# Spacing numbers, two buffer counts and one bank string changed in the hybrid layer of a three-layer kernel

## Chip, core and metric

The kernel runs on one core of one Trainium2 chip. The metric is the device time of one execution in microseconds (us), from the first instruction to the last. The engines are PE (TensorE, matrix products), DVE (VectorE), ACT (ScalarE), POOL (GpSimd) and SP (SyncE, which here only issues DMA transfers).

## What is computed

Three transformer layers run over 256 tokens of width 1024: a layer with sliding-window attention and a dense feed-forward, a layer with forgetting attention and eight experts, and a "hybrid" layer with 32 small experts. Only the hybrid mixer is touched:

```python
def hybrid_mixer(x, ...):
    proj = x @ w_in                                   # 1024 -> 6912 columns
    y_a = rwkv7_mixer(proj[..., :OFF_MOBA], ...)      # recurrence over the tokens, 8 heads of 64
    y_b = moba_attention(q, k, v)                     # attention, 8 heads of 64
    y_c = s5_mixer(proj[..., OFF_SSM:OFF_GATE], ...)  # state space model, 32 groups of 16 channels
    gates = sigmoid(proj[..., OFF_GATE:] + gate_b)    # three gates of 1024 columns
    merged = gates[0] * (y_a @ w_up_rwkv) + gates[1] * (y_b @ w_up_moba) + gates[2] * (y_c @ w_up_ssm)
    return merged @ w_out
```

The recurrence of `rwkv7_mixer` is S <- S*w + (S a) b' + v k', y = S r for each head and token. The kernel does it in chunks of 64 tokens: two blocks of 128 tokens (`tb` 0 and 1), each with two chunks.

## The kernel before

The weights of the whole program stream through SBUF in parts of 128 x 1024 numbers, in the order of a plan that is made ahead. A part is loaded into a raw buffer (tile `wr`), and where it is wanted in two halves, `_split` writes them into a split buffer (tile `ws`): ACT copies the high half (L123), DVE subtracts it and leaves the low half (L124). Four raw and three split buffers are there all the time; `k.room(nraw, nsplit, k.part_b)` adds some for the parts that lie in the plan ahead of `part_b`. A load or a split is issued as soon as a buffer of its kind has been released by the order of the program, so the number of buffers sets how early a split stands in the queues of ACT and DVE. Every engine takes its own queue strictly in order.

A projection (`gemm`) of 512 columns takes 12 PE instructions of 128x512 for each part, 6 for each half of the tokens; below, "dense" rows are those, on `bank_g`. The eight PSUM banks are shared out by letter: in part A `bank_g` (three), `bank_a` (two) and `bank_t` (three), in part B g=4, t=2, y=2.

The hybrid layer has two parts. In each, `weave(main, *sides, lat)` writes one order for all engines from a main generator of dense work and side generators of small dependent steps. A side that says `yield t` is resumed once the program's own count of PE time (`k.pe.us`, a sum by operand shapes, made while the program is built) has grown by `lat * t`. When the main generator is used up, what is left of the sides is written behind it, with nothing between its steps.

- Part A: `weave(dense(), att, states(), lat=1.0)`. Main is the attention's projections (`mb`), the S5 input `u2` (`inputs()`) and the recurrence's inputs (`z2`); the sides are the attention and the S5 scan (L1780 to L1809).
- Part B: `weave(dense2(), r.steps, r.ahead, lat=0.7)`. Main is the gates, the S5 output (`glu`) and two of the three up projections. The sides are the recurrence: `early(tb)` (decays; exponentials L1993 to L1995, a product with `rind`, normalised keys), `late(tb)` (products `rkt` L2042 and `rbt` L2043, then four turns by PE, called T(rt), T(at), T(rkt), T(rbt) here), `recur(tb)` (products rarT x rbT and rarT x rkT, a matrix inverse by levels with L2137 ahead of the first, then for each chunk W, copy L2170, U, copy L2178, state H and output y) and `finish(tb)` (group norm of y, L2216 to L2234, then the turn T(ry)). `r.ahead` is `early(1)`; `r.steps` is all the rest, `finish(0)` being resumed inside `recur(1)`.

Behind part B the up projection of the recurrence's output (`up0`, on tiles `hyr` that T(ry) and two copies fill) and the output projection `o2` follow, and then the 32 experts, whose weights (`wx`) fill large buffers; more of these open once the buffers of `o2` are closed.

Of the kernel before, what the change touches and what calls it, by code (L numbers as in the profile page):

```python
# [385 lines left out]
def through(gen):  # L386
    for _ in gen:
        pass
# [30 lines left out]
def until(ready, *what):  # L419

    n = 0
    while not all(w in ready for w in what):
        n += 1
        assert n < 10000, what
        yield 0.5
# [179 lines left out]
class Attention:  # L605
# [73 lines left out]
    def steps(self, units):  # L679

        def start(u):
            if "prep" in u:
                yield from u["prep"]
            self.scores(u)

        yield from start(units[0])
        self.soft(units[0])
        yield 5.0
        for n, u in enumerate(units):
            more = n + 1 < len(units)  # L690
            if more:
                yield from start(units[n + 1])
            yield 2.0
            self.turn(u)
            if more:
                self.soft(units[n + 1])
            yield 2.0
            self.values(u)
            if "after" in u:
                u["after"]()  # L700
            yield 2.5
# [900 lines left out]
class Ssm:  # L1602
# [47 lines left out]
    def tile(self, shape, name, bufs=1, dt=F32):  # L1650
        return self.pool.tile(shape, dt, name=name, tag=name, bufs=bufs)
# [206 lines left out]
class Rwkv:  # L1858
# [97 lines left out]
    def early(self, tb, tile):  # L1956

        k, nc, row = self.k, self.k.nc, self.row
        z = self.z[:, tb]
        hd = lambda v: v.rearrange("p (h d) -> p h d", h=8)  # L1960
        wide = lambda v: v.rearrange("p (h o) -> p h o", o=1).to_broadcast([128, 8, 64])
        v = self.of[tb] = {}
        g = v["g"] = self.tile([128, 512], "rg", 2)
        PC = v["PC"] = self.tile([128, 4, 2], "rPC", 2)
        nc.scalar.activation(z[:, 1536:1600], z[:, 1536:1600], AF.Tanh)
        nc.scalar.activation(z[:, 1664:1792], z[:, 1664:1792], AF.Sigmoid)
        lt = self.tile([128, 2, 128], "rlt2")
        yield 1.5
        p = k.t()
        for i in range(2):  # L1970
            k.pe.transpose(p[:, i * 128:i * 128 + 128], z[:, 1536 + i * 128:1664 + i * 128], k.ident)
        k.copy(lt, p[:, :256].rearrange("p (i t) -> p i t", i=2))
        yield 1.5
        sw, a, kk = (tile(i) for i in (6, 7, 3))
        p, p2 = k.t(), k.t()
        k.pe.matmul(p, lt[0:64, 0], self.wa[0:64], start=True, stop=True)
        k.pe.matmul(p2, lt[64:128, 0], self.wa[64:128], start=True, stop=True)
        nc.vector.tensor_add(sw, p, row["w0"])
        nc.vector.tensor_add(a, p2, row["a0"])
        nc.scalar.activation(sw, sw, AF.Sigmoid)  # L1980
        nc.scalar.activation(a, a, AF.Sigmoid)
        kv, r = z[:, 512:1024], z[:, 0:512]
        nc.vector.tensor_mul(kk, kv, row["k_k"])
        yield 2.0
        p = k.t()
        k.pe.matmul(p, lt[:, 1], self.g2, start=True, stop=True)
        nc.scalar.copy(g, p)
        yield 2.0
        E = [tile(i) for i in range(3)]
        p, p2 = k.t(), k.t()  # L1990
        k.pe.matmul(p, self.upto, sw, start=True, stop=True)
        k.pe.matmul(p2, self.before, sw, start=True, stop=True)
        nc.scalar.activation(E[0], p, AF.Exp, scale=-KAPPA)  # L1993
        nc.scalar.activation(E[1], p, AF.Exp, scale=KAPPA)
        nc.scalar.activation(E[2], p2, AF.Exp, scale=-KAPPA)  # L1995
        yield 1.5
        p = k.t()
        for j in range(4):
            k.pe.matmul(p[:, 2 * j:2 * j + 2], sw[:, j * 128:j * 128 + 128], self.ind, start=True, stop=True)
        nc.scalar.activation(PC, p[:, :8].rearrange("p (j c) -> p j c", c=2), AF.Exp, scale=-KAPPA)  # L2000

        sq = sw
        nc.gpsimd.tensor_mul(sq, kk, kk)
        yield 1.5
        s8 = self.tile([128, 3, 8], "rs8", 2)
        nc.vector.tensor_reduce(out=s8[:, 0], in_=hd(sq), op=OP.add, axis=AX.X)
        nc.gpsimd.tensor_scalar(s8[:, 0], s8[:, 0], 1e-24, None, op0=OP.max)
        nc.gpsimd.tensor_tensor(s8[:, 1], s8[:, 0], k.neghalf.to_broadcast([128, 8]), op=OP.pow)
        rt, at = E[0], E[2]
        nc.vector.tensor_mul(rt, r, rt)  # L2010

        kn = kv
        nc.vector.scalar_tensor_tensor(sq, a, -1.0, row["k_a"], op0=OP.add, op1=OP.mult)
        nc.vector.scalar_tensor_tensor(kn, sq, 1.0, kv, op0=OP.add, op1=OP.mult)
        yield 3.0
        nc.vector.tensor_mul(hd(kk), hd(kk), wide(s8[:, 1]))
        nc.vector.scalar_tensor_tensor(at, kk, -1.0, at, op0=OP.mult, op1=OP.mult)
        nc.gpsimd.tensor_mul(a, kk, a)
        v.update(rt=rt, at=at, a=a, E=E[1], kn=kn)
        yield 2.0  # L2020
        self.ready.add(tb)

    def late(self, tb):

        k, nc, row = self.k, self.k.nc, self.row
        hd = lambda v: v.rearrange("p (h d) -> p h d", h=8)
        v = self.of[tb]
        self.bt = self.tile([128, 512], "rbt")
        self.kt = self.tile([128, 512], "rkt")
        self.arT = self.tile([128, 4, 2, 128], "rarT")  # L2030
        self.bT = self.tile([128, 4, 128], "rbT")
        self.kT = self.tile([128, 4, 128], "rkT")
        bonus = v["bonus"] = self.tile([128, 8], "rbonus", 2)
        self.PC = v["PC"]

        def turned(src, dst):
            p = k.t()
            for j in range(4):
                k.pe.transpose(p[:, j * 128:j * 128 + 128], src[:, j * 128:j * 128 + 128], k.ident)
            k.copy(dst, p.rearrange("p (j t) -> p j t", j=4))  # L2040

        nc.vector.tensor_mul(self.kt, v["kn"], v["E"])  # L2042
        nc.gpsimd.tensor_mul(self.bt, v["a"], v["E"])  # L2043
        turned(v["rt"], self.arT[:, :, 1])
        yield 1.0
        turned(v["at"], self.arT[:, :, 0])
        yield 1.5
        turned(self.kt, self.kT)
        yield 1.5
        turned(self.bt, self.bT)  # L2050
        kn = v["kn"]
        nc.gpsimd.tensor_mul(kn, kn, row["r_k"])
        nc.gpsimd.tensor_mul(kn, kn, self.z[:, tb, 0:512])
        yield 2.0
        nc.vector.tensor_reduce(out=bonus, in_=hd(kn), op=OP.add, axis=AX.X)

    def steps(self, yh, yl):
        yield from self.early(0, lambda i: self.tile([128, 512], f"ru{i}"))
        yield from self.late(0)
        yield from self.recur(0)  # L2060
        end = self.finish(0, yh, yl)
        next(end)
        yield from until(self.ready, 1)
        yield from self.late(1)
        for i, t in enumerate(self.recur(1)):
            if i in (1, 4):
                next(end, None)
            yield t
        yield from self.finish(1, yh, yl)
# [24 lines left out]
    def recur(self, tb):  # L2094
        k, nc = self.k, self.k.nc
# [30 lines left out]
        def level(l):  # L2126
            t = tl([128, 2, 4, 64], "ru5" if l % 2 else "ru8")
            nc.gpsimd.tensor_mul(f(t), f(NT), lv(self.level[:, l]))
            return t
# [6 lines left out]
        products(MN, lambda u, hs: self.eye[hs], p)  # L2136
        nc.vector.tensor_add(f(X), pv(p), lv(self.eye))  # L2137
        MN = level(1)
        yield 2.0
        for l in range(1, 6):  # L2140
            p = k.t()
            products(MN, lambda u, hs: f(X)[hs, u], p)
# [102 lines left out]
ALPHA2 = 2.0 ** 0.25  # L2245
NIN = 6912
MOBA_BUFS = 1
MORE_A = (2, 0)
LAT_A, LAT_B = 1.0, 0.7
ZCHUNKS = ((1536, 256), (512, 512), (0, 512), (1024, 512))  # L2250

# [101 lines left out]
def hybrid(k, A, x, before, scratch, spare, extra):  # L2353
    nc, tc = k.nc, k.tc
    with ExitStack() as hy:
# [18 lines left out]
        with ExitStack() as pa:  # L2374
# [17 lines left out]
            ep = es.enter_context(k.pool(name="rws", side="right"))  # L2392
            close = k.room(*MORE_A, k.part_b)
            through(islice(g, 2))
# [7 lines left out]
            r.constants()  # L2402

            def inputs():
                ps = [k.bank(b) for b in "gggt"]
                yield from turned_gemm(k, "u2", xh, xl, 512, ps)
                us = ep.tile([128, 4, 4, 64], F32, name="hus")
                for b in range(4):
                    k.copy(us[:, b], ps[b][:, :256].rearrange("p (n t) -> p t n", t=4))
                for h, e in enumerate((nc.vector, nc.gpsimd)):  # L2410
                    for t in range(4):
                        for c in range(4):
                            e.tensor_copy(uT[h][32 * t:32 * t + 32].rearrange("p (b c) n -> p b c n", c=4)[:, :, c],
                                          us[32 * c:32 * c + 32, 2 * h:2 * h + 2, t])
                ready.add("u")
# [507 lines left out]
```

## Time before, and its profile

| | |
|---|---|
| median of 3 runs | 1864.01 us (1863.45 to 1866.99) |
| profiled execution | 1866.05 us, span 1864.3 us |
| mean granted PE clock | 0.971 of full speed |
| PE busy over the span | 1730.8 us, 93% |
| DVE, ACT, POOL busy | 718.0, 455.7, 363.9 us (39%, 24%, 20%) |
| part A (1244 to 1384 us) | 140 us, PE busy 128.64 |
| part B (1384 to 1577 us) | 193 us, PE busy 175.64 |

PE is the busiest engine in every stage shown. Its idle time within a stage is what other engines or transfers make it wait for, and the profile names the instruction that released it.

### The profile page before, as it was taken

The page shows a single profiled execution, that of the slowest core. Times are in us where ns is not written, and L with a number is a line of the kernel's source. Part 1 is how long each engine was busy: PE and PEld are TensorE (multiplying, and loading weights), DVE is VectorE, ACT ScalarE, POOL GpSimd, SP SyncE. Part 2 cuts the span into 40 slices and gives each one's busy share as a digit, 9 for nine tenths or more (in the row PEclk, how much of TensorE's full clock was granted, in tenths as well). Part 3 has the DMA queues.
Part 4 walks back from the last instruction along what each step waited for, and adds up shares of the span by engine and source line. Part 5 has one row for each costly group of instructions (what it writes and reads, how often), then busy time and mean ns, then how long its engine had stood idle before and what let it go on. Part 6 is the DMA issues. An engine that isn't in the chain of part 4 may idle for free. (4 is left out here: it accounts for less than half of the span.)

```text
span 1864.3 us, 41874 instructions
## 1 busy us (share of the span) xinstructions
PE 1730.8 (93%) x18607; PEld 1197.5 (64%) x18607; DVE 718.0 (39%) x1147; ACT 455.7 (24%) x791; POOL 363.9 (20%) x622
## 2 busy tenths in 40 slices
PE   8989999899899999999999999989889989889776
PEld 7867888788645464646464656578767767665343
DVE  5558655654501020202112020247677565621102
ACT  5534444355210000000000000024344333311001
POOL 4410989400100000000000000036234142000000
PEclk9999999999999999999999999989999999989889
DMA  7515676544579999999999999855564235989996
GB/s 226 154 57 186 199 231 207 172 115 165 221 300 381 409 379 405 383 405 384 406 383 394 393 383 405 324 195 162 169 185 130 81 87 168 363 353 419 419 418 233
DMA packets 126483, 514.97 MB, mean 276 GB/s; under 512 B 21148, under 2 KB 50250, under 8 KB 88916
## 3 DMA queue, kind: packets, MB, share of 16 engines
q1 hardware_dynamic: 123012, 496.35, 70.7%
q0 software_dynamic: 3280, 15.83, 2.6%
q8 instruction: 150, 2.46, 0.5%
q14 instruction: 41, 0.34, 0.1%
HBM read 502.44 MB, written 7.87 MB: 274 GB/s over the span
## 5 line engine op out<-in xcount | busy, mean ns | idle before, releaser
L232 PE MATMUL bank_r<-wl,gx 128*32 128x352 f32 x6144 | 459.4, 460 | 2.5 <-ACTq L1357 2.5
L232 PE MATMUL bank_g<-ws,xh 128*128 128x256 f32 (+2 forms) x1440 | 389.4, 351 | 14.5 <-DVE ws L124 5.2
L232 PEld LDWEIGHTS bank_r<-wl,gx 128*32 128x32 f32 x6144 | 217.9, 110 | 237.3 <-issue 140.0
L124 DVE TENSOR_TENSOR ws<-wr,ws 128x1024 fp32r<-128x1024 f32 (+1 forms) x200 | 256.9, 1294 | 156.9 <-ACT ws L123 156.5
L232 PEld LDWEIGHTS bank_g<-ws,xh 128*128 128x128 f32 x1440 | 257.3, 196 | 54.6 <-DVE ws L124 7.9
L123 ACT ACTIVATE ws<-wr 128x1024 fp32r<-128x1024 f32 (+1 forms) x200 | 209.6, 1058 | 205.0 <-PE bank_g L232 113.9
L232 PE MATMUL bank_g<-ws,xl 128*128 128x256 f32 (+2 forms) x720 | 236.2, 344 | 3.3 <-DVE xl L363 3.1
L232 PE MATMUL bank_r<-wl,ehT 128*32 128x256 f32 x4224 | 231.4, 379 | 4.2 <-DVE ehT L1445 4.0
L232 PEld LDWEIGHTS bank_r<-wl,ehT 128*32 128x32 f32 x4224 | 161.2, 110 | 72.2 <-issue 8.9
L1444 DVE TENSOR_TENSOR eh<-eh,bank_r 128x352 f32<-128x352 f32 x48 | 22.9, 504 | 428.7 <-PE bank_r L232 428.1
L566 POOL TENSOR_TENSOR lnmv<-lnmv,neghalf 128x1 f32<-128x1 f32 x10 | 10.0, 1000 | 822.1 <-DVE lnmv L565 822.1
L232 PEld LDWEIGHTS bank_g<-ws,xl 128*128 128x128 f32 x720 | 141.1, 196 | 17.5 <-DVE xl L363 4.1
L1467 ACT CAST ey<-bank_r 128x256 fp32r<-128x256 f32 x24 | 8.9, 373 | 415.5 <-PE bank_r L232 414.6
L232 PE MATMUL bank_g<-wx,x 128*32 128x256 f32 x784 | 71.2, 433 | 15.6 <-DMA wx<-in_expert_w_gate_dram 14.4
L1468 DVE TENSOR_TENSOR ey<-bank_r,ey 128x256 fp32r<-128x256 f32 x24 | 10.1, 424 | 165.0 <-ACT ey L1467 164.9
L1438 ACT ACTIVATE eh<-bank_r 128x352 f32<-128x352 f32 x48 | 22.3, 465 | 206.7 <-PE bank_r L232 201.6
L232 PEld LDWEIGHTS bank_g<-wx,x 128*32 128x32 f32 x784 | 32.7, 123 | 45.6 <-DMA wx<-in_expert_w_gate_dram 19.1
L650 POOL TENSOR_TENSOR aP<-aP,ast 128x512 f32<-128x512 f32 (+1 forms) x20 | 24.4, 1219 | 175.6 <-DVE ast L648 133.9
L232 PE MATMUL bank_g<-ws,hh 128*128 128x512 f32 x176 | 57.5, 399 | 0.0
L232 PE MATMUL bank_g<-ws,oh 128*128 128x512 f32 x128 | 44.4, 409 | 0.0
L1445 DVE STREAM_TRANSPOSE ehT<-eh 128x704 f32<-128x704 f32 x24 | 43.0, 1792 | 0.8
L583 POOL TENSOR_TENSOR lnmv<-lnmv,neghalf 128x1 f32<-128x1 f32 x2 | 1.1, 558 | 205.4 <-DVE lnmv L582 205.4
(715 smaller groups left out, 2202.8 us busy)
## 6 DMA issues: line engine op xcount, KB each, us to landing
wl<-in_w_exp_in_dram SPq DMA_DIRECT2D x128, 1408.0 KB, 8.8
wl<-in_w_exp_out_dram SPq DMA_DIRECT2D x64, 1408.0 KB, 8.4
wr<-in_w_in_dram SPq DMA_DIRECT2D x54, 512.0 KB, 3.8
wx<-in_expert_w_up_dram SPq DMA_DIRECT2D x25, 1024.0 KB, 19.9
wx<-in_expert_w_gate_dram SPq DMA_DIRECT2D x24, 1024.0 KB, 19.9
wx<-in_expert_w_down_dram SPq DMA_DIRECT2D x23, 1024.0 KB, 19.9
wr<-in_w_ffn_in_dram SPq DMA_DIRECT2D x44, 512.0 KB, 4.1
wr<-in_w_out_dram SPq DMA_DIRECT2D x24, 512.0 KB, 4.3
```

The costliest lines, as they stand in the source:

```text
L123: nc.scalar.activation(hv, v, AF.Copy)
L124: nc.vector.tensor_sub(lv, v, hv.bitcast(F32))
L232: self.nc.tensor.matmul(out, lhsT, rhs, start=start, stop=stop)
L566: nc.gpsimd.tensor_tensor(mv[:, 3:4], mv[:, 2:3], self.k.neghalf, op=OP.pow)
L583: nc.gpsimd.tensor_tensor(mv[:, 3:4], mv[:, 2:3], self.k.neghalf, op=OP.pow)
L650: e.tensor_mul(P[:, hs, :nk], P[:, hs, :nk], st[:, 3, hs].rearrange("p (h o) -> p h o", o=1).to_broadcast([128, 2, nk]))
L1438: nc.scalar.activation(h[:, g, s * H2:s * H2 + H2], pa[g][s], AF.Silu)
L1444: nc.vector.tensor_mul(v, v, pb[g][s])
L1445: nc.vector.transpose(hT[:, g], h[:, g].rearrange("p (r j) -> p j r", j=KF))
L1467: nc.scalar.copy(y[:, 0, g], ps[g])
L1468: nc.vector.tensor_sub(y[:, 1, g], ps[g], y[:, 0, g].bitcast(F32))
```

## The change

```diff
--- before.py
+++ after.py
@@ -1993,7 +1993,7 @@
         nc.scalar.activation(E[0], p, AF.Exp, scale=-KAPPA)
         nc.scalar.activation(E[1], p, AF.Exp, scale=KAPPA)
         nc.scalar.activation(E[2], p2, AF.Exp, scale=-KAPPA)
-        yield 1.5
+        yield 8.0
         p = k.t()
         for j in range(4):
             k.pe.matmul(p[:, 2 * j:2 * j + 2], sw[:, j * 128:j * 128 + 128], self.ind, start=True, stop=True)
@@ -2044,9 +2044,9 @@
         turned(v["rt"], self.arT[:, :, 1])
         yield 1.0
         turned(v["at"], self.arT[:, :, 0])
-        yield 1.5
+        yield 4.0
         turned(self.kt, self.kT)
-        yield 1.5
+        yield 4.0
         turned(self.bt, self.bT)
         kn = v["kn"]
         nc.gpsimd.tensor_mul(kn, kn, row["r_k"])
@@ -2063,7 +2063,7 @@
         yield from until(self.ready, 1)
         yield from self.late(1)
         for i, t in enumerate(self.recur(1)):
-            if i in (1, 4):
+            if i in (4, 7):
                 next(end, None)
             yield t
         yield from self.finish(1, yh, yl)
@@ -2136,7 +2136,7 @@
         products(MN, lambda u, hs: self.eye[hs], p)
         nc.vector.tensor_add(f(X), pv(p), lv(self.eye))
         MN = level(1)
-        yield 2.0
+        yield 4.0
         for l in range(1, 6):
             p = k.t()
             products(MN, lambda u, hs: f(X)[hs, u], p)
@@ -2245,7 +2245,7 @@
 ALPHA2 = 2.0 ** 0.25
 NIN = 6912
 MOBA_BUFS = 1
-MORE_A = (2, 0)
+MORE_A = (0, 1)
 LAT_A, LAT_B = 1.0, 0.7
 ZCHUNKS = ((1536, 256), (512, 512), (0, 512), (1024, 512))
 
@@ -2402,7 +2402,7 @@
             r.constants()
 
             def inputs():
-                ps = [k.bank(b) for b in "gggt"]
+                ps = [k.bank(b) for b in "ggtt"]
                 yield from turned_gemm(k, "u2", xh, xl, 512, ps)
                 us = ep.tile([128, 4, 4, 64], F32, name="hus")
                 for b in range(4):
```

Four spacing numbers, a pair of step numbers, a pair of buffer counts and one string change. `yield` values grow in `early` (behind the exponentials), `late` (ahead of T(rkt) and T(rbt)) and `recur` (ahead of the first level's products), and `finish(0)` is resumed at the steps 4 and 7 of `recur(1)` instead of 1 and 4. `MORE_A` gives part A one more split buffer in place of two more raw ones: 4 raw and 4 split instead of 6 and 3. The `u2` projection puts its third block of 128 columns on a `bank_t` instead of a `bank_g`. No instruction is added or removed by it; the order of every engine's queue changes.

The first place is DVE's queue at the start of part A, where the splits begin (`L334` is a copy of attention values; the numbers behind `ws_` and `wr_` only tell tiles apart).

```order
 L363 TENSOR_TENSOR xl<-bank_t,xh 128x4x128 x2
-L124 TENSOR_TENSOR ws_12575<-wr_12041,ws_12575 128x1024
-L124 TENSOR_TENSOR ws_12580<-wr_12565,ws_12580 128x1024
-L124 TENSOR_TENSOR ws_12617<-wr_12567,ws_12617 128x1024
+L124 TENSOR_TENSOR ws_12571<-wr_12041,ws_12571 128x1024
+L124 TENSOR_TENSOR ws_12576<-wr_12565,ws_12576 128x1024
+L124 TENSOR_TENSOR ws_12581<-wr_12567,ws_12581 128x1024
+L124 TENSOR_TENSOR ws_12618<-wr_12569,ws_12618 128x1024
 L334 COPY hmb_12366<-bank_g 128x256
```

Four splits stand ahead of the first copy instead of three, and so on through part A: each split stands one part earlier, until the last one.

The second place is PE's queue at the start of part B, from the two products with `sw` (`rupto`, `rbefore`) on. Before:

```order
L232 MATMUL bank_t<-ru_13808,rupto 128x512
L232 MATMUL bank_t<-ru_13808,rbefore 128x512
L232 MATMUL bank_g<-ws_13797,xh 128x512
L232 MATMUL bank_g<-ws_13797,xl 128x512
L232 MATMUL bank_g<-ws_13797,xh 128x512
L232 MATMUL bank_g<-ws_13797,xl 128x512
L232 MATMUL bank_g<-ws_13797,xh 128x512 x2
L232 MATMUL bank_t<-rind,ru_13808 128x2 x4
```

With the change:

```order
L232 MATMUL bank_t<-ru_13808,rupto 128x512
L232 MATMUL bank_t<-ru_13808,rbefore 128x512
L232 MATMUL bank_g<-ws_13797,xh 128x512
L232 MATMUL bank_g<-ws_13797,xl 128x512
L232 MATMUL bank_g<-ws_13797,xh 128x512
L232 MATMUL bank_g<-ws_13797,xl 128x512
L232 MATMUL bank_g<-ws_13797,xh 128x512 x2
L232 MATMUL bank_g<-ws_13826,xh 128x512
```

The product with `rind`, 6 dense instructions behind `rbefore` in the one, comes 24 dense instructions later in the other. In the same way T(rkt) and T(rbt) have 18 dense instructions ahead of them instead of 6 in both blocks, and the first level's products in the second block 18 in place of 12.

The third place is PE's queue at the end of part B. Before, these rows stand ahead of the last T(ry), and 34 dense instructions more ahead of them, back to the last product of `recur(1)` on `bank_y`:

```order
L232 MATMUL bank_g<-ws_15566,xh 128x512 x2
L232 MATMUL bank_g<-ws_15598,xh 128x512
L232 MATMUL bank_g<-ws_15598,xl 128x512
L232 MATMUL bank_g<-ws_15598,xh 128x512
L232 MATMUL bank_g<-ws_15598,xl 128x512
L232 MATMUL bank_g<-ws_15598,xh 128x512 x2
L236 MATMUL bank_t<-ident,ry 128x128 x4
```

With the change:

```order
L232 MATMUL bank_y<-rUc,ru_15023 64x64
L232 MATMUL bank_y<-rHc,rarT 64x64
L232 MATMUL bank_y<-rz,ru_15025 64x64
L232 MATMUL bank_y<-rUc,ru_15023 64x64
L236 MATMUL bank_t<-ident,ry 128x128 x4
L232 MATMUL bank_g<-ws_15380,hyr_13750 128x512
L232 MATMUL bank_g<-ws_15380,hyr_13751 128x512
```

All dense rows of part B now stand ahead of the last 16 products on `bank_y` of the level steps; from there to T(ry) the recurrence's steps follow each other (W, U, H and y of chunk 0, then W, U and y of chunk 1), and behind T(ry) come `up0`'s rows with `hyr`.

## Rows read from the trace of the kernel before

**Rows 1.** Windows A, B: us; PE, PEld, DVE, ACT, POOL busy us; PE clock, DMA share, GB/s.
```profile
1244.00:1384.00 140.00, 128.64 (x895) 112.66 (x894) 95.69 (x128) 57.42 (x103) 66.02 (x109) 0.98 0.56 179
1384.00:1577.00 193.00, 175.64 (x2026) 136.29 (x2026) 121.70 (x161) 71.40 (x96) 65.87 (x51) 0.98 0.41 126
```

**Rows 2.** Waits of PE from 1270 to 1660: us in all, times, longest us.
```profile
PE bank_g L232 <- DVE ws L124: 5.2, 4, 4.1
PE bank_t L232 <- ACT ru L1994: 4.2, 1, 4.2
PE bank_t L236 <- DVE ry L2234: 3.5, 1, 3.5
PE bank_t L236 <- DVE rkt L2042: 3.1, 2, 1.8
PE bank_g L232 <- ACT hus L332: 2.8, 1, 2.8
PE bank_t L232 <- DVE ru L2137: 2.5, 1, 2.5
PE bank_t L236 <- POOL rbt L2043: 2.3, 1, 2.3
```

**Rows 3.** Timeline of DVE, then PE, around 1340: start, us, engine, line, tile.
```profile
1331.42 1.23 DVE L124 TENSOR_TENSOR ws<-wr,ws 128x1024 fp32r<-128x1024 f32 x1
1337.03 1.52 DVE L1806 TENSOR_TENSOR st<-sq,srot 128x504 f32<-128x504 f32 x1
...
1342.94 1.74 DVE L124 TENSOR_TENSOR ws<-wr,ws 128x1024 fp32r<-128x1024 f32 x1
...
1344.73 0.73 PE L232 MATMUL bank_g<-ws,xh 128*128 128x512 f32 x2 [4.06 <-DVE ws L124]
```

**Rows 4.** Windows of 4 us behind four gaps; columns as in rows 1.
```profile
1344.00:1348.00 4.00, 3.27 (x15) 2.81 (x16) 3.96 (x7) 1.17 (x2) 1.27 (x1) 0.67 0.43 131
...
1496.00:1500.00 4.00, 2.75 (x14) 2.38 (x15) 0.48 (x1) 2.04 (x4) 3.90 (x4) 1.00 0.65 189
1516.00:1520.00 4.00, 4.00 (x37) 3.41 (x33) 2.00 (x3) 2.64 (x4) 0.00 (x0) 0.57 0.35 122
1576.00:1580.00 4.00, 2.94 (x10) 2.49 (x11) 3.76 (x5) 0.17 (x1) 0.00 (x0) 0.69 0.22 53
```

**Rows 5.** Timeline of DVE and PE behind the u2 projection.
```profile
1281.01 5.19 DVE L2413 COPY huT<-hus 32x128 f32<-32x128 f32 x16
...
1287.82 2.34 PE L232 MATMUL bank_t<-huT,sBT 128*128 128x64 f32 x20
```

**Rows 6.** Timeline of PE and DVE at the start of part B.
```profile
1416.22 3.02 PE L232 MATMUL bank_g<-ws,hy 128*128 128x512 f32 x12
...
1417.43 0.68 DVE L334 COPY rbT<-bank_t 128x512 f32<-128x512 f32 x1
```

**Rows 7.** Timeline of PE, ACT, DVE and POOL at the end of part B.
```profile
1563.55 0.28 PE L232 MATMUL bank_y<-rUc,ru 64*64 64x64 f32 x2
...
1564.43 0.63 ACT L2216 COPY ry<-bank_y 128x256 f32<-128x256 f32 x2
...
1565.70 0.68 DVE L2221 TENSOR_REDUCE rgn<-ry 128x8 f32<-128x512 f32 x1
...
1570.49 1.67 POOL L2227 TENSOR_TENSOR rgn<-rgn,neghalf 128x8 f32<-128x8 f32 x1
...
1572.19 1.53 DVE L2231 TENSOR_TENSOR ry<-ry,rgn 128x512 f32<-128x512 f32 x1 [1.84 <-POOL rgn L2227]
...
1577.06 0.69 PE L236 MATMUL bank_t<-ident,ry 128*128 128x128 f32 x4 [3.50 <-DVE ry L2234]
```

**Rows 8.** Window of H and y of chunk 0, second block; columns as in rows 1.
```profile
1552.89:1555.53 2.64, 2.64 (x81) 2.57 (x81) 1.07 (x3) 0.00 (x0) 0.00 (x0) 1.00 1.01 425
```

**Rows 9.** All instructions of line L2170 in part B: duration min/median/max in ns.
```profile
L2170 DVE COPY rWc<-bank_t x4: 417/421/425, 1469.2 to 1558.4; 128x256 f32<-128x256 f32 x4
```

**Rows 10.** The chain that ended last, near its end: start, us, what.
```profile
1842.36 7.08 DMA wx<-in_expert_w_down_dram
```

## The prediction

> **What bounds the kernel now.** I read the stages first. In part A PE is busy for 128.64 of 140 us, in part B for 175.64 of 193 us, and no other engine comes near that [rows 1]. So a stage gets shorter only where PE waits, and 11.4 and 17.4 us are all there is to win. The table of PE's waits then says for what: seven causes hold most of it, each once or a few times [rows 2]. The reader should see that none of them is a transfer; all are results of DVE, ACT or POOL that come late for one row of PE's queue. Last I looked at where the hybrid layer's end goes. The chain of waits ends with a load of expert weights of 7.08 us [rows 10], and those loads are released by PE as it finishes with the buffers; so I let a shift of part B's end pass one to one to the end of the program.
>
> A second cost hangs on the waits. Behind the gap of 2.50 us the granted clock is 0.57 over the next 4 us, behind the one of 4.06 us 0.67, behind the one of 3.50 us 0.69, and behind the one of 2.35 us it is 1.00 [rows 2 to 4]. A window at 0.57 has lost 4 x 0.43 = 1.7 us of full-speed work, one at 0.67 1.3 us. So I count a gap of 2.5 us or more as its length and 1.3 to 1.7 us on top, and a shorter one as its length alone.
>
> **The change part by part.** No instruction is added, so the sum is made of waits that go, waits that come and the clock behind both.
>
> *The split buffer.* The longest split wait of part A is at 1344.73: PE has waited 4.06 us for a low half (L124) that starts at 1342.94, because on DVE it stands behind four operations of the S5 scan that began at 1337.03; the split before it ran at 1331.42 [rows 3]. With each split one part earlier, the half that PE wants at 1340.7 stands in the place of the one at 1331.42. The next half, which runs at 1342.94, is wanted only after the rest of that part and the S5 and attention products that PE's order has there, which need the scan's end themselves; I leave 0.3 us for that. Gain 3.8 us, and 1.3 us of clock: -5.1. Bounds: nothing (another split waits in its place, see below) and -5.8 (with the 1.7 us of clock). The two raw buffers that go cost nothing: a raw part is split as soon as it is there, the wait table names no load of `wr`, and DMA is busy at 0.56 [rows 1]; should that cover fail, one exposed split load would cost no more than the wait just removed.
>
> *The shared banks.* PE waits 2.8 us for ACT to copy a `bank_g` of `u2` [rows 2]. With a `bank_g` more at hand the next projection starts at once. But the S5 products that follow need `huT`, whose 16 copies on DVE run from 1281.01 for 5.19 us to 1286.2, and PE reached them at 1287.82 [rows 5]. PE can't pass 1286.4, so the gain is at most 1.4 us; the rest of the wait only moves there. I take -1.4; the lower bound is 0. The two parts of part A: -6.5.
>
> *Start of part B.* PE waits 4.2 us for the exponentials (L1994) and 1.8 us for `rkt` [rows 2], 6.0 in all, with a low clock behind the first. The change puts 24 dense instructions ahead of the `rind` product and 12 each ahead of T(rkt) and T(rbt). Twelve take 3.02 us [rows 6], so this is 6.0 + 3.0 + 3.0 us of cover, more than the waits are long. Against it: the dense rows that move bring their own splits with them, each 1.2 us of DVE [rows 3], ahead of the very operations the recurrence waits for. Three low halves instead of one stand ahead of the normalisation of the keys, and gate and S5 output sums (0.7 us each) come in ahead of L2017 and of the copy of `rbT` (L334, 0.68 us [rows 6]), for which the first product rarT x rbT waits. Walking DVE's and ACT's queues with the durations of the profile I find new waits of 1.4 us (a split behind the exponentials), 1.3 us at T(at), 1 us at T(rkt), 0.6 us in small pieces and 3.2 us ahead of rarT x rbT: 7.5 us against 6.0 + 1.7. I take 0. Bounds: -7.7 (every wait hidden) and +3.5 (the 3.2 us is a gap that brings the low clock and the rest grows by 2).
>
> *Second block.* Here `rkt` costs 1.23 us (3.1 less 1.85), `rbt` 2.3 and the first level (L2137) 2.5 with 1.7 of clock [rows 2, 4]. The dense rows put ahead are 3.0 us for each of the first two and 1.5 us for the third, whose own wait also starts from an emptier DVE queue. I take -3.1 for the two and -3.9 for the third, leaving 0.8 us of small waits: -7.0. Bounds -7.8 and -3.5 (cover of 1.5 us only for the third, the clock still falling behind the first two).
>
> *The end of part B.* The rows put ahead were taken from somewhere: the order has no dense row left between the last level step and T(ry). Two things are then bare. First the finish chain: from the last product of y, which ends at 1563.83, to T(ry) at 1577.06 it took 13.2 us [rows 7]: two copies on ACT, seven operations on DVE, three on POOL, one behind the other. It was covered by 42 dense rows, which is why PE waited only 3.50 us. With no split in DVE's and ACT's queues the copies start some 0.5 us sooner and L2221 follows them 0.4 us sooner: 12.3 us. Second, four copies between the last products, 0.42 us each [rows 9] and about 0.2 us to pass on the result and back, which dense rows covered: 2.5 us. Together 14.8 us bare for 3.5 before: +11.3; the low clock behind T(ry) is the same as now (0.69, [rows 4]). Bounds: +8 (the chain is a quarter shorter when nothing runs beside it: L2231 took 1.53 us where L2221, which reads as many numbers, took 0.68 [rows 7]) and +17 (below).
>
> *Sum:* -6.5 + 0 - 7.0 + 11.3 = -2.2 us. The profiled execution took 1866.05 us (its span of 1864.3 and 1.75 around it), so it would take 1863.85. It was 2.04 above the median of 1864.01; against the median I forecast 1861.8 us.
>
> **The rivals.** *The waits at the start of part B go too.* For it speaks that 12 us of cover stand against 6.0 us of waits and DVE is busy for only 121.70 of 193 us [rows 1]; against it, the order of DVE's queue, which puts splits and gate sums ahead of the wanted results. Then 6 of the 7.7 us are saved as well: 1855.8 us.
>
> *Slower: the bare end runs at the low clock.* From the last level step on PE has short products with gaps between them, which the trace nowhere shows for so long. H and y of the first chunk hold PE for 2.64 us [rows 8]; W and U of both chunks, y of the second and the last level step are about twice that again, so some 8 us at full clock (an estimate). If most of that runs at half speed it costs 6 us more, and with the 3.2 us gap at the start of part B followed by a low clock, 1.7: -2.2 + 7.7 = +5.5, 1869.5 us. It decides once more than about half of those products run slow. The page "TensorE: Matmul & The Clock Gate" of the Trainium skill, section "Loop structure matters more than you think", warns of just such a loop: it has the array go cold in a long wait between bursts and the next products run at the lower of the two clocks. By that rule alone the small products between short copies would stay fast and only the rows behind the 12 us gap be slow, as they are now; the trace agrees as far as it goes, with 0.69 behind 3.50 us and 1.00 behind 2.35 us.
>
> *Part A's stall only moves.* If the split at 1342.94 is still the one PE needs next, because the S5 products come later than I read, PE waits there instead: -5.1 becomes -1, and the sum +1.9: 1865.9 us.
>
> **How the numbers follow.** Forecast 0.45 (own range 1858.5 to 1865), first rival 0.2, second 0.2, third 0.15. A measurement of this kernel can tell about 0.2%, 3.7 us, from no change. Faster than 1860.3: the first rival and 0.35 of the forecast, 0.36. Slower than 1867.7: most of the second, a fifth of the third and a little of the forecast, 0.25. The rest, 0.39, is within 0.2%. The range leaves out one in ten on each side: 1854.5 to 1870.
>
> **What would show it.** In the profile after: no wait of 4 us for L124 in part A, and no window at 0.67 behind it; `huT` products reached some 1.4 us sooner, counted from `u2`; no wait for L1994, but new ones for L334 `rbT` in part B's first 45 us; no wait for `rbt` and at most 0.5 us for L2137; and one wait of 11 to 13 us for `ry` L2234 ahead of the last T(ry), with short ones for L2170 and L2178 ahead of it. I am wrong if that last wait is under 8 us, if the clock falls before it, or if the end of part B moves and the end of the program doesn't, because loads of expert weights set it by themselves.

## The result and the profile after

The changed kernel takes 1871.22 us in the median of 20 runs (1866.15 to 1881.61), the kernel before 1861.02 us in 20 runs on the same chips. The ratio is 1.0059, with a 95% interval of 1.0049 to 1.0070: slower, by some 11 us, where I had forecast 2.2 us less and a range that ended at 1870. The profiled execution has a span of 1873.0 us. The ratios and mean clocks below leave out two runs far off the rest (2467.70 us of a control, 5947.83 us of the kernel before).

The table of PE's waits from 1240 to 1660 us (in all, times, longest), to be laid beside [rows 2]:

```profile
PE bank_t L236 <- DVE ry L2234: 11.0, 1, 11.0
PE bank_g L232 <- ACT xxT L374: 6.5, 1, 6.5
PE bank_t L232 <- DVE ru L2113: 5.1, 1, 5.1
PE bank_g L232 <- DVE hmb L334: 4.2, 2, 2.3
PE bank_t L232 <- DVE hy L677: 3.9, 1, 3.9
...
PE bank_t L232 <- DVE rbT L334: 2.7, 1, 2.7
```

Every wait of [rows 2] that the change was aimed at is gone or smaller, and new ones stand in their places. The second row is the largest of those that no part of the prediction has. It lies behind part B, in the router of the experts (lines L2599 to L2623), which the diff does not touch. Timelines of ACT, SP and PE there in the changed kernel:

```profile
1635.65 2.02 ACT L2613 COPY xp<-x 128x1024 f32<-128x1024 f32 x1 [16.34 <-DVE x L571]
1637.58 1.06 ACT L374 COPY xxT<-bank_t 128x512 f32<-128x512 f32 x2
...
1628.54 0.58 SPq L2599 DMA_DIRECT2D xwr<-in_router_expert_w_dram  x1
1634.74 0.34 SPq L2602 DMA_DIRECT2D xrows<-in_ln_w_dram  x1
...
1635.79 1.28 SPq L192 DMA_DIRECT2D wx<-in_expert_w_gate_dram  x3
...
1638.21 2.13 PE L232 MATMUL bank_g<-xxT,xwr 128*36 128x128 f32 x9 [6.47 <-ACT xxT L374]
```

and in the kernel before:

```profile
1622.92 2.06 ACT L2613 COPY xp<-x 128x1024 f32<-128x1024 f32 x1 [9.89 <-DVE x L571]
...
1621.52 0.58 SPq L2599 DMA_DIRECT2D xwr<-in_router_expert_w_dram  x1
1622.20 0.62 SPq L2602 DMA_DIRECT2D xrows<-in_ln_w_dram  x1
...
1625.52 1.94 PE L232 MATMUL bank_g<-xxT,xwr 128*36 128x128 f32 x16
```

Before, the load of `xrows` follows that of `xwr` at once, and the copy follows the norm of the first 128 tokens. In the changed kernel ACT's copy of x into `xp` and SP's load of `xrows` both stand still until 1635, when DVE has finished the norm of the second 128 tokens. Behind ACT's copy queue the copies to `xxT` that PE wants, behind SP's load all further loads of expert weights.

To see where time goes I cut each trace at five places: the last copy L362 (part A begins), the first turn of `rz` by PE (part B's recurrence begins), the last T(ry), the load of `xrows`, and `xM` (the routing is known); a stage ends where the instruction named starts. The kernel before is a mean of three traces, one shown ahead and two controls:

| stage, us | before (3) | changed | overlap alone (2) | spacing alone (2) | all, one raw more |
|---|---|---|---|---|---|
| up to part A | 1245.9 | 1248.7 | 1245.3 | 1242.0 | 1243.8 |
| part A | 137.3 | 141.5 | 137.4 | 137.4 | 141.4 |
| part B to T(ry) | 196.3 | 199.9 | 195.8 | 200.8 | 200.1 |
| up0 and o2 to the xrows load | 44.0 | 44.7 | 49.7 | 38.3 | 38.8 |
| router to xM | 14.3 | 16.0 | 15.8 | 14.3 | 13.6 |
| experts | 225.0 | 222.3 | 224.1 | 225.9 | 225.5 |

The program ahead of part A and the experts vary by 3 and 5 us from run to run in the same kernel (1244.2 to 1247.3 and 222.9 to 227.8 in the three of before; ahead of part A, which the change does not touch, 1238.8 to 1248.7 over all fourteen traces), each of the four stages between by less than 1.5. Over these four the changed kernel takes 402.1 us for 391.9, 10.1 us more, about what the times say.

### The profile page after: what moved, and what is told of

It reads as the page before. It is cut to its first block, busy times and chain, and to the rows that moved or that the text cites. A ratio compares the mean times of both kernels' runs of the same rounds, so it can differ in the third digit from the quotient of the medians.

```text
span 1873.0 us, 41874 instructions
## 1 busy us (share of the span) xinstructions
PE 1728.0 (92%) x18607; PEld 1200.9 (64%) x18607; DVE 719.8 (38%) x1147; ACT 453.7 (24%) x791; POOL 365.3 (20%) x622
## 5 line engine op out<-in xcount | busy, mean ns | idle before, releaser
L124 DVE TENSOR_TENSOR ws<-wr,ws 128x1024 fp32r<-128x1024 f32 (+1 forms) x200 | 260.2, 1312 | 161.6 <-ACT ws L123 161.0
L1468 DVE TENSOR_TENSOR ey<-bank_r,ey 128x256 fp32r<-128x256 f32 x24 | 10.1, 424 | 164.8 <-ACT ey L1467 164.7
```

What stands on the lines that cost most here:

```text
L124: nc.vector.tensor_sub(lv, v, hv.bitcast(F32))
L1468: nc.vector.tensor_sub(y[:, 1, g], ps[g], y[:, 0, g].bitcast(F32))
```

## The experiments

The theory, formed on the two traces: the buffer counts lose the time, and they do it behind part B. The four raw buffers of the stream take turns. Two extra ones in part A or none leave the turn at another place when part A ends, and with it every later part lies in another buffer, up to the norm's weight and bias (L570 and L571 read them). Where the tiles lie in SBUF, from the two built programs (bytes in a partition, from and to):

```
before   norm weight wr4 16736-20832   norm bias wr3 20832-24928
changed  norm weight wr2 24928-29024   norm bias wr1 29024-33120
both     xrows 25472-25536             xp 25600-33792
```

In the changed kernel `xrows` and `xp` are put where the norm's weights lie, and must wait for the norm's last readers. The rival: the bare end of part B, 11.0 us of waiting for `ry`, is the loss, and the late wait is absorbed, since the experts wait for their weights anyway.

**The overlap alone**, `MORE_A` being the only edit. With three extra raw buffers the turn ends as in the changed kernel, while part A keeps its split buffers.

```diff
-MORE_A = (2, 0)
+MORE_A = (3, 0)
```

> The kernel before with three more raw buffers in part A instead of two (7 raw, 3 split): only the turn of the raw buffers shifts, so that the norm's weights lie under xp and xrows as in the changed kernel. Theory 1: a wait of 5 to 7 us for xxT appears and the first big load of expert weights is issued 5 to 8 us later; ratio 1.002 to 1.004. Theory 2: the wait appears but the end does not move; ratio 0.999 to 1.001.

Ratio 1.0057 (1.0043 to 1.0071), above the range of either theory. I ran it again on another chip, beside a control.

> The overlap variant once more. Its trace showed 6.5 us more up to the routing, its times 10.6 us more. If the router's tiles waiting for the norm is the loss, ratio 1.003 to 1.006 again, whatever the control does; if the first comparison was off by what the others were, 1.003 to 1.004.

Ratio 1.0057 again (1.0040 to 1.0074). PE's waits from 1580 to 1660 us in the second trace, and SP's timeline:

```profile
PE bank_g L232 <- ACT xxT L374: 6.7, 2, 6.5
...
1620.84 0.58 SPq L2599 DMA_DIRECT2D xwr<-in_router_expert_w_dram  x1
1627.75 0.34 SPq L2602 DMA_DIRECT2D xrows<-in_ln_w_dram  x1
```

The same 6.5 us of PE and a gap of 6.3 us between the two loads on SP, while part A and part B stay within 0.5 us of before: in the table it is 5.6 us up to the load and 1.5 in the router. In the built program the norm's weights lie where they do in the changed kernel. In time it is as much as the whole change. The rival fails here: the wait is not absorbed.

**The whole change without the overlap.** One raw buffer more in part A shifts the turn once again.

```diff
-MORE_A = (0, 1)
+MORE_A = (1, 1)
```

> The whole change, but with one raw buffer more in part A (5 raw, 4 split instead of 4 and 4). This shifts the turn of the raw buffers, so that the weights of the norm behind o2 no longer lie where the router's tiles xp and xrows are put. Theory 1 (two side effects of the buffer counts are the loss: the first loads of part A come late, and xp and xrows wait for the norm): the 6.5 us wait for xxT and the 5.5 us wait of the row load on SP go, the 1.9 us wait at part A's start shrinks; 6 to 10 us off the whole change, ratio to the kernel before 1.000 to 1.003. Theory 2 (the bare end of part B, 11.0 us of PE waiting for ry, is the loss, and the late wait is absorbed by the expert weights anyway): no change, ratio 1.005 to 1.007.

Ratio 1.0018 (1.0008 to 1.0029). The norm's weights lie where they did before, the wait for `xxT` and the gap on SP are gone while `ry` is still waited for 11.0 us, and 0.4% of the 0.6% are gone with them. Part A keeps its 4.1 us. The overlap alone (0.57%) and the change without it (0.18%) come to more than the whole (0.59%); with intervals of 0.1% on each side that is not clear of noise.

**Parts alone.** The split buffer without the overlap (5 raw and 4 split on the kernel before):

```diff
-MORE_A = (2, 0)
+MORE_A = (1, 1)
```

> The kernel before with 5 raw and 4 split buffers in part A instead of 6 and 3, without the overlap behind o2. By the prediction's step the 4.06 us wait for a low half in part A and the low clock behind it go: 5 us off, ratio 0.997. By the new theory the wait only moves to the S5 products (for hy L677, near 4 us, as in the changed kernel), and one raw buffer fewer costs 0 to 2 us at the start of part A: ratio 0.9995 to 1.001.

Ratio 1.0026 (1.0013 to 1.0039), above both ranges, while the four stages of its trace take 391.8 us for 391.9. Its waits of PE in part A:

```profile
PE bank_t L232 <- DVE hy L677: 3.9, 1, 3.9
PE bank_g L232 <- ACT hus L332: 2.8, 1, 2.8
```

The 4.06 us for L124 [rows 3] are gone, and 3.9 us for `hy` L677 have come. Part A is 138.3 us long, 1.0 more than before. DVE's timeline there:

```profile
1340.10 1.20 DVE L1809 TENSOR_TENSOR sS<-sS,st 128x504 f32<-128x504 f32 x1
1341.23 1.74 DVE L124 TENSOR_TENSOR ws<-wr,ws 128x1024 fp32r<-128x1024 f32 x1
...
1343.75 0.41 DVE L677 TENSOR_TENSOR hy<-bank_t,hy 128x256 fp32r<-128x256 f32 x1
```

The bank string:

```diff
-                ps = [k.bank(b) for b in "gggt"]
+                ps = [k.bank(b) for b in "ggtt"]
```

> The kernel before with the third block of u2 on bank_t (ggtt for gggt). By the prediction's step: 1.4 us off, ratio 0.999. By what part A took in two variants (4.2 us longer with the bank string and 5 raw buffers, 1.0 us longer with 5 raw buffers and the old string): 3 us longer, the wait for hus shrinks from 2.8 to 1.3 us and one of 2.3 us for hmb L334 comes, with a low clock behind it; ratio 1.001 to 1.002.

Ratio 1.0006 (0.9987 to 1.0026); part A 136.6 us, 0.7 less. The wait for `hus` shrinks from 2.77 to 1.34 us and one of 2.25 us for `hmb` comes, as the second theory in the expectation had it, but the clock does not fall behind it in this trace, so its 3 us are not there.

The five spacing edits without the two others:

> The whole change without the buffer counts and the bank string: only the five spacing edits. Theory 1: part B grows by about 3.6 us up to the last T(ry), and the up and output projections behind it get some 6 us shorter, since their splits are made in the bare 11 us: ratio 0.997 to 1.000. Theory 2: the bare end costs its whole 8 to 11 us, ratio 1.004 to 1.006.

Ratio 1.0026 (1.0014 to 1.0037), between the two theories. The trace shows the four stages 1.2 us shorter than before, the times 5 us longer; so I ran it again, with the controls.

> The spacing variant once more, on another chip and beside a control: its trace showed the hybrid layer 1.4 us shorter, its times 4.8 us longer. If the trace is right, ratio 0.998 to 1.001 and the same as the control; if the times are, 1.002 to 1.003.

Ratio 1.0015 (1.0005 to 1.0025). PE's waits in it from 1244 to 1590 us:

```profile
PE bank_t L236 <- DVE ry L2234: 11.0, 1, 11.0
PE bank_t L232 <- DVE ru L2113: 5.0, 1, 5.0
PE bank_g L232 <- DVE ws L124: 4.1, 1, 4.1
PE bank_g L232 <- ACT hus L332: 2.8, 1, 2.8
PE bank_t L232 <- DVE rbT L334: 2.7, 1, 2.7
```

Part B is 4.5 us longer and the stage behind it 5.8 us shorter, in the mean of both traces. Of the five edits, the one behind the exponentials by itself:

```diff
         nc.scalar.activation(E[2], p2, AF.Exp, scale=-KAPPA)
-        yield 1.5
+        yield 8.0
```

> The kernel before with only the yield behind the exponentials raised from 1.5 to 8.0: 24 dense instructions are put ahead of the rind product. The wait of 4.2 us for L1994 and the low clock behind it go (5.9 us); what is taken from the end of part B bares up to 5 us more of the finish chain. If moving dense work only moves the idle time: ratio 0.999 to 1.001. If the freed clock counts: 0.997 to 0.999.

Ratio 1.0004 (0.9988 to 1.0020): the 4.2 us for L1994 are gone, but one of 3.6 us for `ru` L2128 (POOL) comes and `ry` L2234 is waited for 6.3 us instead of 3.5; part B is 4.4 us longer and the stage behind it 2.8 us shorter. The bare end the other way round, with more cover than before:

```diff
         nc.vector.tensor_mul(y, y, g)
-        yield 4.0
+        yield 14.0
...
                 for i, _ in enumerate(gate(0, gt)):
...
+                first.extend(w[0] for w in k.st.get(*((("up", 0, 0), p) for p in range(2))))
+                up0(0, 0)
+                yield
...
```

(The rest of the edit, which takes this quarter out of its old place behind part B, is left out here.)

> The kernel before with the first quarter of up0 (12 dense instructions, for the tokens and columns whose inputs are long ready) put into part B ahead of the last T(ry), which is delayed behind all of part B's dense work. Nothing is left out. If bare time in front of T(ry) counts, the wait of 3.5 us for ry L2234 and the low clock behind it go: 3 to 5 us off, ratio 0.997 to 0.9985. If the end of part B is made up for behind it anyway, as in the spacing variant: ratio 0.999 to 1.001.

Ratio 1.0006 (0.9991 to 1.0022). No wait for `ry` is left in the trace, but PE waits 2.2 and 2.1 us for the two halves of `hyr` behind T(ry) (L2242, L2241): the idle time moved by one step. And the spacing and the bank string together:

> The whole change except for the buffer counts: spacing and bank string changed, 6 raw and 3 split buffers in part A as before. If the buffer counts carry the whole loss (the norm's weights under xp and xrows, and part A longer): part A about 137 us, part B and what follows it about 239 us for 240.5, ratio 0.998 to 1.001. If the spacing costs 0.26% as its first comparison said: 1.002 to 1.003.

Ratio 1.0014 (1.0001 to 1.0026), against 1.0059 with the buffer counts; part A takes 136.5 us.

**Controls**, the kernel before against itself:

> The kernel before, unchanged. Its use is to see how far a second copy of the same program differs from the runs that it is compared with, and to have a second trace of it. Both theories: ratio 1.000, within 0.1%. Should it come out at 1.002 or more, the 0.2% of the three variants without the overlap are not theirs.

> The kernel before, unchanged, beside the others of this call. Ratio 0.999 to 1.001.

Ratios 0.9993 (0.9978 to 1.0008) and 1.0004 (0.9989 to 1.0019). So the 0.57% of the overlap stands clear of what two copies of one program differ by, the 0.15 to 0.26% of spacing and split buffer only just. No version beat the kernel before.

## Why the prediction was wrong

Over the four stages the forecast of -2.2 us and the measured +10.1 us lie 12.3 us apart. Part A makes 10.7 of it (-6.5 forecast, +4.2 measured) and the overlap behind part B 8.2 (the two stages there take 60.7 us in the changed kernel and 52.4 with one raw buffer more, one trace of each); part B is 0.7 us below the forecast, and what lies behind it, without the overlap, 5.9 us below. So two steps failed.

**The first step that failed** is the sentence "The two raw buffers that go cost nothing". It asked whether loads would come late, and not what else the number of buffers sets. It sets which buffer each later part falls into, and so which tile of the next stage lies over a tile that is still read. That is 7 us in the trace and 10.6 us in the times of the overlap variant, and without it the change measures +0.18% instead of +0.59%. The order of the changed program, which I had, showed it: the copy L2613 waits for two more DMA queues and `xrows` for one more, and both for a later point of DVE's queue. I compared the order of the instructions as far as T(ry) and not what they wait for behind it. The loads themselves did come late as well: on ACT at the start of part A in the changed kernel

```profile
1263.40 1.06 ACT L123 ACTIVATE ws<-wr 128x1024 fp32r<-128x1024 f32 x1 [4.26 <-DMA wr<-in_w_in_dram]
```

for which PE then waits 1.89 us for `hmb`, because its copy on DVE stands behind the low half of that split and of the next. With one raw buffer more this wait is 0.8 us, as in the kernel before.

**The second step that failed** is the split buffer's "Gain 3.8 us, and 1.3 us of clock: -5.1". The last rival came true: the stall only moved, though not to the next split as I had put it. The S5 products do follow at once, but on `bank_t`, whose last reader `hy` L677 stands on DVE behind the same scan and a split: 3.9 us for 4.06. Alone it is +1.0 us in part A.

**The shared banks, -1.4 forecast.** -0.7 alone, within the bounds. Part A is 4.1 to 4.2 us longer where both edits are in, but not for one reason. In the changed kernel PE is idle there for 13.0 us instead of 10.8, 1.1 us of it by the late load, and the clock is low behind the 1.89 us wait. With one raw buffer more PE's idle time is 11.4 us, and the clock is the larger part. Windows of 4 us from the 2.26 us wait for `hmb` on in that variant:

```profile
1304.66:1308.66 4.00, 2.31 (x15) 2.08 (x17) 2.77 (x4) 0.27 (x1) 0.00 (x0) 0.86 0.69 168
1308.66:1312.66 4.00, 4.00 (x23) 2.70 (x22) 0.00 (x0) 0.78 (x1) 0.00 (x0) 0.50 1.03 407
1312.66:1316.66 4.00, 4.00 (x28) 3.83 (x27) 1.03 (x2) 0.00 (x0) 0.00 (x0) 0.79 0.22 84
```

and from the 2.25 us wait at the same place on, with the bank string alone:

```profile
1299.70:1303.70 4.00, 3.40 (x28) 2.62 (x28) 1.68 (x3) 1.06 (x1) 0.00 (x0) 1.00 0.81 269
1303.70:1307.70 4.00, 4.00 (x35) 3.76 (x35) 0.99 (x2) 0.00 (x0) 0.00 (x0) 1.00 0.88 352
```

The first three have lost 4 x (0.14 + 0.50 + 0.21) = 3.4 us of full speed, the others none. In the changed kernel itself the wait at this place is 2.28 us, and the clock stays up:

```profile
1313.70:1317.70 4.00, 3.98 (x32) 3.14 (x33) 1.09 (x1) 1.06 (x1) 0.00 (x0) 1.00 0.89 293
```

So the two kernels lose the same 4 us in different ways, and that the sums agree looks like chance.

**Part B, 0 - 7.0 + 11.3 = +4.3 forecast, +3.6 measured**, by errors that cancel. At its start the 3.2 us for `rbT` came as 2.7, the rest of the 7.5 us as 1.8, with no wait for L1994 or `rkt`: about 3 us better than I took it. In the second block the three waits went as forecast, but one of 5.1 us for L2113 came that I had not. DVE's timeline in the spacing variant:

```profile
1514.56 0.69 DVE L2055 TENSOR_REDUCE rbonus<-rz 128x8 f32<-128x512 f32 x1 [2.51 <-POOL rz L2053]
...
1516.42 1.42 DVE L2113 TENSOR_TENSOR ru<-bank_t,rmask 128x256 f32<-128x256 f32 x4
```

L2113, which frees the banks that PE wants, stands on DVE behind a sum that waits for POOL, with three short copies between. At the end the chain is bare for 11.0 us and the small copies for 1.9 us, 12.9 for the forecast 14.8. The 0.2 us that the prediction adds to each copy stand in no row; the four waits are 0.42 to 0.52 us each, hardly more than the copy's own 0.42.

**Behind part B, 0 forecast, -5.2 to -5.8 measured** from T(ry) to the `xrows` load where the overlap does not hide it (38.3 and 38.8 us for 44.0). Windows from the last T(ry) to that load, the kernel before and the spacing variant:

```profile
1577.42:1622.20 44.78, 40.76 (x166) 30.98 (x165) 28.82 (x37) 14.03 (x17) 1.00 (x1) 0.92 0.90 352
...
1579.70:1617.99 38.29, 36.13 (x159) 28.81 (x159) 25.84 (x33) 12.89 (x15) 1.00 (x1) 0.97 0.87 329
```

In the mean of the traces the 5.8 us of the spacing variant are 1.4 us of shorter waits (PE idle for 2.2 us instead of 3.6), some 2.4 us of clock (44 x 0.08 against 38.3 x 0.03), and some 2 us less of PE's own work. The last is no gain: six dense rows, 1.5 us by [rows 6], stand ahead of T(ry) now instead of behind it. The clock is better because it is low during the long wait itself (0.50 from 1573 to 1579 us in the spacing variant) and not at all in `o2`, where before it is 0.50 once more, behind a wait of 1.6 us. That ACT and DVE split ahead during the wait can explain the 1.4 us of shorter waits and no more. My rule of one to one for the end of part B was wrong by the 3.8 us of waits and clock, against 9.4 us more of bare time. More cover in front of T(ry) gained nothing for another reason: the wait came back at `hyr`.

**The rival of the low clock in the bare end** did not come to pass. Windows of the changed kernel over the last products ahead of the 11.0 us wait, and behind it (the clock is the third figure from the end):

```profile
1574.00:1578.30 4.30, 3.31 (x103) 3.00 (x97) 0.85 (x2) 0.04 (x1) 0.00 (x0) 1.00 0.02 4
...
1589.40:1593.40 4.00, 3.99 (x13) 3.38 (x14) 1.99 (x3) 2.49 (x3) 0.00 (x0) 0.59 0.80 279
```

The short products with copies between them ran at full clock, and only what follows the long gap ran slow. The trace agrees here with the rule of the Trainium skill that the prediction cites ("TensorE: Matmul & The Clock Gate", section "Loop structure matters more than you think").

**What stays open.** The times say that the spacing costs 0.15 to 0.26%, the trace of the four stages says -1.2 us; the split buffer costs 0.26% with four stages as long as before, and the overlap 3 to 4 us more than its trace. The profiled executions of the controls lie 4.3 and 3.7 us above their own medians, those of the spacing variants 4.2 and 1.9 us below. The mean granted clock, on record for every run, says what the missing part goes with:

| mean granted clock of the runs | variant | kernel before beside it |
|---|---|---|
| spacing, first and second comparison | 0.9686, 0.9691 | 0.9725, 0.9718 |
| split buffer alone | 0.9688 | 0.9725 |
| overlap alone, first and second | 0.9668, 0.9672 | 0.9725, 0.9718 |
| controls | 0.9705, 0.9708 | 0.9715, 0.9718 |

Among the runs of the kernel before, a clock 0.001 lower goes with 1.0 to 1.3 us more (an estimate, by a straight line through each of three sets of runs). By that the 0.0027 to 0.0039 of the spacing and the split buffer are 3 to 5 us, all that their times show. The profiled executions miss it because they are single draws: 0.972 in the first spacing variant, 0.966 in the first control. A difference of 0.001, some 1.1 us, comes without any edit, as the controls show. In which part of the program the other executions lose the clock, and whether the edits cause all of it, no trace here shows.

## What to carry to other kernels

A buffer count in a ring is not local: it sets where the turn stands when the stage ends, and every later tile moves with it. After such an edit compare, to the end of the program, what the instructions wait for, and not only their order; a new wait on a first copy or a first load of the next stage is the thing to look for. And before idle time in front of one instruction is given a price, follow it to the end of the next stage: here 1.4 us of 9.4 came back as shorter waits and 2.4 in the clock.

## What the hardware showed that I had not expected

Whether PE's granted clock falls behind a gap does not follow from the gap's length alone, at 1.9 to 2.8 us. Windows of the changed kernel behind the 1.89 us wait for `hmb` and behind the 2.67 us wait for `rbT`:

```profile
1267.50:1271.50 4.00, 3.96 (x22) 3.73 (x23) 1.12 (x1) 0.00 (x0) 3.54 (x10) 0.61 0.89 273
...
1436.70:1440.70 4.00, 3.96 (x46) 3.27 (x48) 3.97 (x10) 0.00 (x0) 0.00 (x0) 1.00 0.50 148
```

The shorter gap was followed by the low clock, the longer was not. At one place in part A four traces have a gap of 2.25 to 2.28 us (the bank string alone, with the spacing, in the changed kernel, and there with one raw buffer more): the clock fell in the last alone. It also differs between executions of one kernel: windows of 12 us behind the wait for L1994, in the kernel before (4.18 us of wait) and in the first control (4.38 us):

```profile
1398.90:1410.90 12.00, 12.00 (x54) 9.91 (x55) 7.08 (x9) 8.00 (x10) 5.65 (x5) 0.86 0.32 92
...
1401.20:1413.20 12.00, 11.79 (x41) 9.72 (x42) 6.41 (x9) 7.09 (x9) 5.43 (x5) 0.66 0.32 90
```

The one has lost 12 x 0.14 = 1.7 us, the other 12 x 0.34 = 4.1 us. I had counted on a bound of 2.5 us, and on 1.3 to 1.7 us above it. A gap of about 2 us cost its own length or up to 3.4 us more, and an estimate should carry both. The same page of the Trainium skill, section "What's actually happening", says of the slow matmuls at a kernel's start that their number varies from run to run, because the chip's watch on PE's activity runs free of the program. The windows above show such a variation behind gaps within a kernel, which fits it; no run here shows the reason.
